# Moving one copy of weight sums to the row unit's loads, and one weight tile ahead of the last chunk's sums, in a decoder layer kernel

## Chip, cores and metric

The kernel runs on one core of one Trainium2 chip. The metric is the device time of one execution in microseconds (us). Engines are named as the profile names them: PE (matmul), DVE (VectorE), ACT (ScalarE), POOL (GpSimd), SP (SyncE, which here only issues DMAs).

## What is computed

A decoder layer on x of shape (1, 256, 1024) in float32. Two parallel head groups, a pooled mixer and a causal attention, share an input projection; then comes a cross-attention into 256 memory tokens; then a SwiGLU feed-forward with 2816 hidden columns. Each is followed by a layer norm. The change lies in the feed-forward:

```python
def swiglu(h, w_gate, w_up, w_down):
    return (jax.nn.silu(h @ w_gate) * (h @ w_up)) @ w_down

h = layer_norm(DEEPNORM_ALPHA * h + swiglu(h, w_gate[l], w_up[l], w_down[l]),
               ln3_g[l], ln3_b[l])
```

## The kernel before

**Two parts of every weight.** Float32 products are made from reduced-precision operands. Each weight tile w is split into a high part, `wNh`, an ACT cast of the raw tile `wNr` (L160), and a low part, `wNl`, a DVE subtraction raw minus high (L176). PE then does three products per pair: high by high, high by low, low by high (`three`, L484 to L486; for gate and up L499 and L505). So every weight tile passes SP (load), ACT (cast), DVE (subtract) and PE, in that order. The class `Stream` numbers the tiles 0 to 150 in the order of their use. A raw tile has one of 7 buffers, and SP loads the next tile as soon as DVE has subtracted the tile that held the buffer; split tiles have 10 slots at this stage. `ws.more()` casts and splits one tile ahead of its use, if a slot is free; while `ws.held` is true, nothing is split ahead on its own. `ws.before(n, load)` hangs another load in front of tile n's load on SP's queue.

**Saved products.** Several weight matrices are multiplied by a scheme with seven products of quarters instead of eight (names y, z, w and o are a tile's place in it). The scheme needs sums of weight quarters. DMAs make them in DRAM: `begin_sums(i)` (L435) copies a third of two quarters of down's weights, 1.5 MB, from the input to `sum_z`, and `begin_second(i)` (L440) copies 0.75 MB to `sum_w`, both on SP's queue. Then POOL issues two accumulating DMAs (`add_to`, L447): `add_first(i)` adds other quarters to `sum_z`, and `add_second(i)`, once the first has landed, adds `sum_z` to `sum_w`. `add_first(1)` is issued behind tile 97's cast, `add_first(2)` behind tile 112's cast (`behind`, L428, a small POOL addition that reads the tile). The copies' places are set by one table:

```python
for i, (at, then) in enumerate(((c_gu[1][0], c_gu[1][2]), (c_gs[0]["o"], c_gs[0]["w"]), (c_gu[9][2], c_gu[9][3]))):
    ws.before(at, lambda i=i: begin_sums(i))
    ws.before(then, lambda i=i: begin_second(i))
```

**The feed-forward's order.** Gate and up are done in 11 chunks of 256 columns. Chunks 1 to 4 and 7 to 10 have four tiles each and 64 matmuls (`proj_both`); chunk 10 has tiles 111 to 114, chunk 9 tiles 107 to 110. Chunks 5 and 6 are one "row unit" (`Rows.products`) in four groups with tiles 85 to 98; its third group has tiles 92 (y), 93 (o), 94 (w) and 95 (z), its fourth 96 to 98. After a chunk's matmuls, `Gated.add` takes its four results from PSUM: an ACT copy (L1349) and a DVE addition (L1350) each, called the chunk's sums here. While the next chunk's matmuls run, `multiply` (ACT silu L1354, DVE product L1355) and `split` (three DVE additions L734 to L736, an ACT cast L1368, a DVE subtraction L1375) make the chunk's input for down. Down's weights are tiles 115 to 150. Its first products, of tiles 115 and 116, use PSUM banks that chunk 9 has left; the products of tile 117 need banks that chunk 10's sums set free.

Every engine takes its instructions in the order of the program.

Of the kernel before, what the change touches and what calls it, by code (L numbers as in the profile page):

```python
# [24 lines left out]
NFC = DFF // CW  # L25
# [18 lines left out]
ROWS = (5, 6)  # L44
# [178 lines left out]
def decoder_layer(  # L223
# [78 lines left out]
    c_gu, c_gs = {}, [{} for _ in range(KD // 2)]  # L302
# [122 lines left out]
    def behind(number):  # L425

        hi = r32(ws.tiles[number][0][:, 0, 0:1])
        nc.gpsimd.tensor_add(token, hi, hi)  # L428
# [3 lines left out]
    def begin_sums(i):  # L432
        sums_begun.add(i)
        js = slice(i * THIRD, (i + 1) * THIRD)
        nc.sync.dma_start(sum_z[:, :, js], w_sum[:, 1:3, js])  # L435

    def begin_second(i):
        sums_begun.add(~i)
        js = slice(i * THIRD, (i + 1) * THIRD)
        nc.sync.dma_start(sum_w[:, js], w_sum[:, 1, js])  # L440

    for i, (at, then) in enumerate(((c_gu[1][0], c_gu[1][2]), (c_gs[0]["o"], c_gs[0]["w"]), (c_gu[9][2], c_gu[9][3]))):
        ws.before(at, lambda i=i: begin_sums(i))
        ws.before(then, lambda i=i: begin_second(i))

# [3 lines left out]
    def add_first(i):  # L449
        assert i in sums_begun  # L450
        js = slice(i * THIRD, (i + 1) * THIRD)
        add_to(sum_z[:, :, js], w_sum[:, 2:4, js])

    def add_second(i):
        assert ~i in sums_begun
        js = slice(i * THIRD, (i + 1) * THIRD)
        add_to(sum_w[:, js], sum_z[:, 1, js])
# [33 lines left out]
    def proj_both(pss, numbers, yT, group=KD):  # L491

        for k0 in range(0, KD, group):
            for k in range(k0, k0 + group):
                hi, _ = ws.get(numbers, k)
                for b, ps in enumerate(pss):
                    nc.tensor.matmul(ps, hi[:, b * P:(b + 1) * P], yT.both(k), start=k == 0, stop=False,  # L499
                                     skip_group_check=True)  # L500
                yield
            for k in range(k0, k0 + group):
                _, lo = ws.parts_of(numbers, k)
                for b, ps in enumerate(pss):
                    nc.tensor.matmul(ps[:, S:], lo[:, b * P:(b + 1) * P], yT.pair(k)[0], start=False,  # L505
                                     stop=k == KD - 1, skip_group_check=True)
                ws.done(numbers, k)
                if ws.pace == 1:
                    ws.next()
                yield  # L510
# [31 lines left out]
    def run(gen, n=None):  # L542

        while n is None or n > 0:
            if next(gen, gen) is gen:
                return False
            n = None if n is None else n - 1
        return True
# [778 lines left out]
    def gated_t():  # L1327
        pt = bank("pgt").rearrange("p (f t) -> p f t", f=2)
        for t in range(T):
            for f in range(2):  # L1330
                nc.tensor.transpose(pt[:, f, t * P:(t + 1) * P], sg0[:, t, f * P:(f + 1) * P], ident)
        gated_parts(0)
        split(gT[0][0], gT[0][1], pt.rearrange("p f (t s) -> p (f t) s", t=T))
# [179 lines left out]
    for c in range(1, NFC):  # L1513
        if c == ROWS[0]:
            run(more_forms)
            rows = Rows()
            ws.lazy = c_gu[ROWS[-1] + 1][2:]
            gu = rows.products()
            run(gu, 3)
            left.multiply()  # L1520
            run(gu, 5)
            ws.apart = True
            run(gu, 1)
            left.split()
            run(gu, 7)
            ws.held = True
            run(gu)
            behind(c_gs[3]["w"])
            add_first(1)
            add_second(1)  # L1530
            left = rows
        if c in ROWS:
            continue
        pss = [(accbank if c % 2 else bank)("pg") for _ in range(4)]
        if c == 3:
            ws.ahead += 1
            ws.widen("spare", sp)
            add_second(0)
        if c == 10:
            behind(c_gu[10][1])  # L1540
            add_first(2)
            add_second(2)
        ws.held = ws.held or c in (ROWS[0] - 1, NFC - 1)
        gu = proj_both(pss, c_gu[c], h2T, KD if c == 1 else 4)
        run(gu, 2)
        if left:
            left.multiply()
        if left and left is rows:
            ws.prepare(c_gu[c][-1] + 1)
        run(gu, 2)  # L1550
        if left and left is rows:
            run(gu, 3)
            left.transposed()
            left.split()
            ws.held = False
        elif left:
            left.split((more_forms, 4 - c) if c in (2, 3) else None)
            if c == 2:
                run(more_forms, 2)
            if c == ROWS[-1] + 2:  # L1560
                run(later)
        else:
            run(gu, 4)
            gated_t()
        if c >= 2:
            run(gu, 7 if c < ROWS[0] else 4 if c == ROWS[-1] + 1 else 0)
            if c < ROWS[0] - 1:
                run(more_forms, 1)
            if c == ROWS[0] - 1:
                ws.more()  # L1570
            ws.held = True
        run(gu)
        left = Gated(c, pss)
        left.add()
        ws.held = False
# [174 lines left out]
```

## Time and profile before

| | us |
|---|---|
| median of 3 runs (378.67, 379.5, 378.67) | 378.67 |
| the profiled execution's own time | 379.65 |
| its span in the profile | 377.9 |
| PE busy / DVE busy / ACT busy / POOL busy | 364.5 / 341.9 / 231.3 / 37.3 |

The profile is of one execution. Its times are from the start of the span; a row of a timeline has start, duration, engine, line, operation and tile, with the engine's idle time before it in brackets, and the engine that ended that. "DMA to landing" is the time from an issue to its completion. A matmul row is longer than the pitch between matmuls, since they are pipelined; the pitch is read from the starts. "q1" is the queue of the DMAs that SP issues, "q0" that of POOL's accumulating ones; both run on the core's 16 DMA engines.

### The profile page before, as it was taken

How to read it: one execution, taken by the hardware profiler on the slowest of the kernel's cores; microseconds unless marked ns; L12 is line 12 of the kernel's file. 1: busy time of each engine (PE TensorE's matmuls, PEld its weight loads, DVE VectorE, ACT ScalarE, POOL GpSimd, SP SyncE). 2: the span in 40 equal slices, each digit the busy share in tenths (PEclk: the TensorE clock that was granted, in tenths of full speed). 3: DMA queues.
4: the chain of work that ended last, by engine and by line, in shares of the span. 5: the costliest groups of instructions: out<-in, count | busy, mean ns of one | idle time of the engine just before them, and what ended most of it. 6: DMA issues, size and time to landing. Idle time of an engine off the chain costs nothing.

```text
span 377.9 us, 5500 instructions
## 1 busy us (share of the span) xinstructions
PE 364.5 (96%) x1941; PEld 309.2 (82%) x1941; DVE 341.9 (90%) x523; ACT 231.3 (61%) x356; POOL 37.3 (10%) x43
## 2 busy tenths in 40 slices
PE   8999999999999999999999999999999998899991
PEld 7887878888888899988888888888988875688880
DVE  5878998999999899899869999999977998999995
ACT  5767768658272865774467675775646475777611
POOL 0000145700130001001100000020000100000002
PEclk9999999999999999999999999999999999899997
DMA  7999999769869999999999996389999998899402
GB/s 267 414 409 357 236 366 289 273 234 294 342 117 257 377 361 340 245 363 343 264 248 333 375 316 209 114 280 230 370 327 378 211 325 290 274 367 301 180 0 112
DMA packets 33755, 107.58 MB, mean 285 GB/s; under 512 B 3264, under 2 KB 4544, under 8 KB 32320
## 3 DMA queue, kind: packets, MB, share of 16 engines
q1 hardware_dynamic: 31056, 93.41, 68.2%
q0 software_dynamic: 2240, 13.37, 18.3%
q10 hardware_dynamic: 432, 0.46, 0.3%
q8 instruction: 15, 0.25, 0.3%
q14 instruction: 12, 0.10, 0.1%
HBM read 106.18 MB, written 27.79 MB: 355 GB/s over the span
## 4 chain that ended last, share of the span: by engine, by line
PE 70%; DVE 16%; DMA 6%; issue 3%; ACT 3%; SPq 0%; DVEq 0%; ACTq 0%
PE pg L499 8%; PE pg L505 4%; PE pxq L499 4%; PE pxk L499 4%; PE pqk L618 4%; DMA w110r<-in_w_gu 3%; PE m L485 3%; PE m L486 3%; PE m L484 3%; PE x L484 2%; PE x L486 2%; PE x L485 2%; PE pxk L505 2%; PE pxq L505 2%; PE pu L499 2%
## 5 line engine op out<-in xcount | busy, mean ns | idle before, releaser
L1368 ACT CAST g<-sq 128x1024 fp32r<-128x1024 f32 x7 | 7.4, 1052 | 14.6 <-DVE sq L736 14.6
L923 POOL TENSOR_TENSOR rs<-mv,mhalf 128x1 f32<-128x1 f32 x6 | 3.8, 640 | 101.5 <-DVE mv L921 101.5
L683 ACT ACTIVATE pr<-pr,mx 128x128 f32<-128x128 f32 (+1 forms) x16 | 7.1, 445 | 7.7 <-DVE mx L714 7.7
L1375 DVE TENSOR_TENSOR g<-sq,g 128x1024 fp32r<-128x1024 f32 x7 | 8.6, 1224 | 1.1 <-ACT g L1368 1.1
L1354 ACT ACTIVATE sq<-sq 128x512 f32<-128x512 f32 x8 | 5.1, 640 | 5.4 <-DVE sq L1350 5.4
L912 DVE BATCH_NORM_STATS2 st<-r 128x6 f32<-128x512 f32 (+1 forms) x12 | 8.1, 671 | 0.4
L577 ACT ACTIVATE h2f<-tp,turned 128x128 f32<-128x128 f32 x8 | 3.0, 456 | 7.0 <-PE tp L574 7.0
L928 DVE SCALAR_TENSOR_TENSOR r<-r,mv,gb 128x512 f32<-128x512 f32 (+2 forms) x10 | 6.9, 726 | 0.1
L428 POOL TENSOR_TENSOR token<-w97h 128x1 f32<-128x1 f32 x1 | 1.0, 963 | 60.6 <-ACT w97h L160 60.6
L1349 ACT COPY sq<-pg 128x256 f32<-128x256 f32 x16 | 5.1, 371 | 2.6 <-DVE g L1375 1.3
L1350 DVE TENSOR_TENSOR sq<-pg,sq 128x256 f32<-128x256 f32 x16 | 6.0, 417 | 0.7 <-ACT sq L1349 0.7
L1029 DVE TENSOR_TENSOR r<-r,u 128x512 f32<-128x512 f32 x6 | 6.0, 1009 | 0.1
L826 ACT CAST xkTh<-pxk 128x256 fp32r<-128x256 f32 x8 | 2.6, 377 | 5.6 <-PE pxk L505 5.6
L1350 DVE TENSOR_TENSOR sg<-pg,sg 128x256 f32<-128x256 f32 x16 | 6.0, 414 | 0.0
L939 ACT ACTIVATE h<-r,rs 128x512 f32<-128x512 f32 x2 | 1.3, 716 | 7.3 <-DVE r L928 7.3
L1355 DVE TENSOR_TENSOR sq<-sq,sg 128x512 f32<-128x512 f32 x8 | 5.5, 687 | 0.3
L683 ACT ACTIVATE xpr<-xs,mx 128x256 f32<-128x256 f32 x6 | 2.8, 470 | 4.8 <-DVE mx L694 4.8
L783 POOL TENSOR_TENSOR win<-upad 128x542 f32<-128x542 f32 x2 | 4.0, 1994 | 16.3 <-DVE upad L816 16.3
L447 POOL DMA_DIRECT2D sum_w<-sum_z x3 | 2.6, 853 | 28.8 <-DMA sum_z<-in_w_sum 28.8
L1349 ACT COPY sg<-pg 128x256 f32<-128x256 f32 x16 | 5.3, 392 | 0.0
L1034 DVE TENSOR_TENSOR r<-m,r 128x512 f32<-128x512 f32 (+1 forms) x8 | 5.2, 649 | 0.1
L1113 PE MATMUL xs<-xkTh,xq 128*128 128x256 f32 x24 | 4.8, 282 | 0.0
(1375 smaller groups left out, 1395.2 us busy)
## 6 DMA issues: line engine op xcount, KB each, us to landing
sum_z<-in_w_sum SPq DMA_DIRECT2D x3, 1536.0 KB, 14.6
sum_z<-in_w_sum POOLq DMA_DIRECT2D x3, 1536.0 KB, 15.2
sum_w<-in_w_sum SPq DMA_DIRECT2D x3, 768.0 KB, 14.8
sum_w<-sum_z POOLq DMA_DIRECT2D x3, 768.0 KB, 9.8
gs_z<-in_w_gs SPq DMA_DIRECT2D x1, 2048.0 KB, 9.8
gs_z<-in_w_gs POOLq DMA_DIRECT2D x1, 2048.0 KB, 17.8
wr<-in_w_qkv SPq DMA_DIRECT2D x5, 256.0 KB, 5.6
mr<-in_mem_t SPq DMA_DIRECT2D x1, 1024.0 KB, 11.3
```

The costliest lines, as they stand in the source:

```text
L484: nc.tensor.matmul(ps, wa, ya, start=start, stop=False, skip_group_check=part)
L485: nc.tensor.matmul(ps, wa, yb, start=False, stop=False, skip_group_check=part)
L486: nc.tensor.matmul(ps, wb, ya, start=False, stop=stop, skip_group_check=part)
L499: nc.tensor.matmul(ps, hi[:, b * P:(b + 1) * P], yT.both(k), start=k == 0, stop=False, skip_group_check=True)
L505: nc.tensor.matmul(ps[:, S:], lo[:, b * P:(b + 1) * P], yT.pair(k)[0], start=False, stop=k == KD - 1, skip_group_check=True)
L618: nc.tensor.matmul(qk[i], part(i)[0], xT.both(k), start=first, stop=False, skip_group_check=True)
L683: nc.scalar.activation(dst[:, j, :], src[:, j, :], AF.Exp, bias=mx[:, j:j + 1], scale=sign, accum_out=sm[:, j:j + 1])
L912: nc.vector.bn_stats(self.st[:, self.n, :], self.r[:, c0:c1] if src is None else src)
L1349: nc.scalar.copy(y[:, f, :], ps[:, S:])
L1350: nc.vector.tensor_add(y[:, f, :], ps[:, :S], y[:, f, :])
L1368: nc.scalar.copy(hi[:, :n], q[:, :n])
L1375: nc.vector.tensor_sub(lo[:, :n], q[:, :n], r32(hi[:, :n]))
```

## The change

Two edits. The third pair of copies (i = 2) hangs no longer in front of tiles 109 and 110 (chunk 9), but in front of tiles 94 and 95 (the row unit's third group). And in chunk 10, `ws.more()` is called ahead of the point where the stream is held, as it was in chunk 4 only; it casts and splits tile 118.

```diff
-    for i, (at, then) in enumerate(((c_gu[1][0], c_gu[1][2]), (c_gs[0]["o"], c_gs[0]["w"]), (c_gu[9][2], c_gu[9][3]))):
+    for i, (at, then) in enumerate(((c_gu[1][0], c_gu[1][2]), (c_gs[0]["o"], c_gs[0]["w"]), (c_gs[2]["w"], c_gs[2]["z"]))):
         ws.before(at, lambda i=i: begin_sums(i))
         ws.before(then, lambda i=i: begin_second(i))
...
-            if c == ROWS[0] - 1:
+            if c in (ROWS[0] - 1, NFC - 1):
                 ws.more()
             ws.held = True
```

On SP's queue, at the row unit's third group, stands now (w92r to w96r are raw tiles, `in_w_gs`, `gs_w` and `gs_z` the row unit's weights and their sums in DRAM):

```order
 L108 DMA w92r<-in_w_gs 128x2x512
 L108 DMA w93r<-in_w_gs 128x1024
+L435 DMA sum_z<-in_w_sum 256x1x1536
 L105 DMA w94r<-gs_w 128x512
+L440 DMA sum_w<-in_w_sum 128x1536
 L108 DMA w95r<-gs_z 128x2x512
 L108 DMA w96r<-in_w_gs 128x2x512
```

The two copies come ahead of tiles 94 and 95; the tiles' own order is as it was.

On the same queue at chunk 9 (`in_w_gu` are gate's and up's weights) stands:

```order
 L108 DMA w107r<-in_w_gu 128x1024
 L108 DMA w108r<-in_w_gu 128x1024
-L435 DMA sum_z<-in_w_sum 256x1x1536
 L108 DMA w109r<-in_w_gu 128x1024
-L440 DMA sum_w<-in_w_sum 128x1536
 L108 DMA w110r<-in_w_gu 128x1024
 L108 DMA w111r<-in_w_gu 128x1024
```

Tiles 109 and 110 follow tile 108 with nothing between.

On DVE at the end of chunk 10 (`go` is chunk 9's input for down, `sq` and `sg` on `pg` are chunk 10's sums) stands:

```order
 L176 TENSOR_TENSOR w117l<-w117r,w117h 128x1024
 L1375 TENSOR_TENSOR go<-sq,go 128x512
-L1350 TENSOR_TENSOR sq<-pg,sq 128x256 x2
-L1350 TENSOR_TENSOR sg<-pg,sg 128x256 x2
 L176 TENSOR_TENSOR w118l<-w118r,w118h 128x1024
+L1350 TENSOR_TENSOR sq<-pg,sq 128x256 x2
+L1350 TENSOR_TENSOR sg<-pg,sg 128x256 x2
 L165 TENSOR_TENSOR w120r<-w119r,w120r 128x512
 L176 TENSOR_TENSOR w119l<-w119r,w119h 128x1024
 L176 TENSOR_TENSOR w120l<-w120r,w120h 128x1024
-L1355 TENSOR_TENSOR sq<-sq,sg 128x512
 L176 TENSOR_TENSOR w121l<-w121r,w121h 128x1024
```

Tile 118's subtraction passes the four sums; behind it the stream stays one tile further ahead, so that chunk 10's product L1355 follows tile 121 and its additions L734 to L736 follow tile 123. ACT's casts move in the same way. The instructions are the same in number on every engine.

## The prediction

> **What bounds the kernel now.** I read the page first, then busy time by stretch, the chain of waits, and the timelines of DVE, PE and SP around the change.
>
> ```profile
> span 377.9 us, 5500 instructions
> ```
>
> Busy time by stretch (stretch; sum of PE, PE's weight loads, DVE, ACT, POOL with counts; granted clock; share of the 16 DMA engines; GB/s):
>
> ```profile
> 228.00:250.00 22.00, 22.00 (x121) 19.15 (x120) 21.23 (x31) 15.12 (x22) 0.00 (x0) 1.00 0.55 170
> 280.00:290.00 10.00, 10.00 (x60) 8.92 (x60) 4.96 (x8) 3.79 (x4) 0.00 (x0) 1.00 1.02 397
> 310.00:320.00 10.00, 9.13 (x36) 6.27 (x36) 8.82 (x14) 5.82 (x8) 0.00 (x0) 1.00 0.92 266
> 320.00:326.00 6.00, 3.68 (x9) 2.69 (x10) 6.00 (x7) 3.88 (x5) 0.00 (x0) 0.73 0.73 250
> 326.00:358.00 32.00, 32.00 (x141) 26.27 (x140) 30.92 (x30) 23.51 (x25) 0.00 (x0) 1.00 0.86 299
> ```
>
> Four things are to be seen. The DMA engines are full in 280 to 290, in chunk 9, and little over half used in 228 to 250, around the row unit's start. In 280 to 290 DVE works only 4.96 of 10 us, while PE does not feel it yet. PE pays later: in 310 to 326 it starts 45 matmuls in 16 us, where at the pace of 326 to 358 (141 in 32 us, 0.227 us each) 45 take 10.2 us. So 5.8 us of PE is lost there, partly as waits, partly as a clock of 0.73. And in 326 to 358 DVE is busy 30.92 of 32 us: it has no spare time in which to catch up.
>
> The chain of waits, asked for 264 to 324, has the load of tile 110 as its longest piece, with its cast behind it; asked for the whole span, it goes on with tile 150's subtraction and DVE's work of the last norm to the end (start, duration, what):
>
> ```profile
> 273.35 12.67 DMA w110r<-in_w_gu
> 286.04 1.06 ACT w110h L160
> ```
>
> ```profile
> 357.15 1.22 DVE w150l L176
> 358.37 0.60 DVE r L1008
> ...
> 372.52 0.75 DVE r L933
> ```
>
> DVE's timeline shows what the late tiles hold up:
>
> ```profile
> 284.02 1.23 DVE L176 TENSOR_TENSOR w109l<-w109r,w109h 128x1024 fp32r<-128x1024 f32 x1 [3.10 <-ACT w109h L160]
> 287.12 1.23 DVE L176 TENSOR_TENSOR w110l<-w110r,w110h 128x1024 fp32r<-128x1024 f32 x1 [1.87 <-ACT w110h L160]
> 309.36 0.75 DVE L1350 TENSOR_TENSOR sq<-pg,sq 128x256 f32<-128x256 f32 x2
> 310.69 1.21 DVE L176 TENSOR_TENSOR w118l<-w118r,w118h 128x1024 fp32r<-128x1024 f32 x1
> 311.82 0.68 DVE L165 TENSOR_TENSOR w120r<-w119r,w120r 128x512 f32<-128x512 f32 x1
> ```
>
> Tiles 109 and 110 land late, behind the third pair of copies on the same queue, and DVE idles 3.10 + 1.87 = 4.97 us. From there on DVE is behind PE and is the path: it reaches chunk 10's sums at 309.36, and from 311.82 on it runs almost without a gap, and at the end its work of the norm follows on tile 150's.
>
> **The copies leave chunk 9.** Landing times of the copies (first two lines: the second pair, with only loads beside it; next two: the third pair), of tile 108, and the slowest load in the whole trace; then each queue's bytes in MB and share in 274 to 280, when POOL's accumulate is on the engines too:
>
> ```profile
> sum_z<-in_w_sum SPq DMA_DIRECT2D x1, 1536.0 KB, 9.4
> sum_w<-in_w_sum SPq DMA_DIRECT2D x1, 768.0 KB, 11.3
> ...
> sum_z<-in_w_sum SPq DMA_DIRECT2D x1, 1536.0 KB, 14.6
> ...
> sum_w<-in_w_sum SPq DMA_DIRECT2D x1, 768.0 KB, 16.5
> ...
> w108r<-in_w_gu SPq DMA_DIRECT2D x1, 512.0 KB, 7.3
> ...
> w73r<-in_w_gu SPq DMA_DIRECT2D x1, 512.0 KB, 21.4
> ```
>
> ```profile
> q0 software_dynamic: 139, 0.78, 63.3%
> q1 hardware_dynamic: 198, 0.94, 40.1%
> ```
>
> ```profile
> 266.59 0.33 SPq L108 DMA_DIRECT2D w108r<-in_w_gu  x1
> ```
>
> Tile 108 lands at 266.59 + 7.3 = 273.9. Without copies, tiles 109 and 110 (0.52 MB each) come next. The loads' queue moved 0.94 MB in 274 to 280, so both are down at about 280.5. DVE wants 109 at 284.02 - 3.10 = 280.9 and 110 one subtraction later, each with a cast of 1.06 us before it. So little or nothing of the 4.97 us is left, and I take nothing; 1 us of it could stay at no cost, as comes next.
>
> **What is late next: PE.** PE runs dense through chunk 10, and its end does not move. PE's and DVE's rows of chunk 4 show how long after the start of the last eight matmuls a chunk's sums can begin; then the last eight of chunk 10:
>
> ```profile
> 240.87 1.12 PE L505 MATMUL pg<-h2T,w84l 128*128 128x256 f32 x8
> ...
> 305.34 1.12 PE L505 MATMUL pg<-h2T,w114l 128*128 128x256 f32 x8
> ```
>
> ```profile
> 242.07 0.76 DVE L1350 TENSOR_TENSOR sq<-pg,sq 128x256 f32<-128x256 f32 x2 [0.18 <-ACT sq L1349]
> 242.75 0.75 DVE L1350 TENSOR_TENSOR sg<-pg,sg 128x256 f32<-128x256 f32 x2
> ```
>
> That is 242.07 - 240.87 = 1.20 us, so chunk 10's sums begin no sooner than 305.34 + 1.20 = 306.54. DVE would be there at 309.36 - 4.97 = 304.39, and would wait 2.15 us.
>
> **Tile 118 ahead of the sums** fills 1.13 us of that wait (310.69 to 311.82): DVE arrives at 305.52, 1.02 us early. This is the slack that a rest of the old stall could use up. ACT's cast of 118 passes the sums likewise, in time in which ACT, too, waits for PE. If the old stall stayed whole, the same subtraction would only put the sums 1.13 us later and cover nothing, at no change in DVE's total.
>
> **The sum.** In chunk 4 the four additions end at 242.75 + 0.75 = 243.50, 1.43 us after their start. So chunk 10's end at 306.54 + 1.43 = 307.97, and the addition for tile 120, which begins at 311.82 now, begins there: 3.85 us earlier. Behind it stand the same instructions (L1355 and L734 to L736 in other places among them), with PE ahead of DVE's needs and every load issued when DVE frees a buffer; I carry the 3.85 us to tile 150 and, since the chain there is DVE's, through the last norm. PE could give 5.8 us, so DVE sets the gain. The profiled execution's own time is 379.65, its span 377.9: 1.75 us lie around the span and stay. 379.65 - 3.85 = 375.8. The profiled execution is 0.98 us above the median of the runs; from the median, 378.67 - 3.85 = 374.8.
>
> **The copies come to the row unit.** SP issues `sum_z` behind tile 93 and `sum_w` behind tile 94; DVE and ACT want tiles 94 and 95 here:
>
> ```profile
> 227.99 0.33 SPq L108 DMA_DIRECT2D w93r<-in_w_gs  x1
> ...
> 233.59 0.52 SPq L108 DMA_DIRECT2D w95r<-gs_z  x1
> ```
>
> ```profile
> 246.12 0.69 DVE L165 TENSOR_TENSOR w94r<-w92r,w94r 128x512 f32<-128x512 f32 x1
> 249.60 1.22 DVE L176 TENSOR_TENSOR w95l<-w95r,w95h 128x1024 fp32r<-128x1024 f32 x1
> 255.72 1.22 DVE L176 TENSOR_TENSOR w98l<-w98r,w98h 128x1024 fp32r<-128x1024 f32 x1
> ```
>
> ```profile
> 257.72 0.39 PE L485 MATMUL g<-w98l,extra 128*128 128x512 f32 x1
> ```
>
> The copies start at about 228.4 and, just ahead of tile 95, at 232.9. By the landings 9.4 to 14.6 and 11.3 to 16.5 they are down at 237.8 to 243.0 and 244.2 to 249.4, and the tile behind each 1.3 us later (0.52 MB at 397 GB/s): 94 at 239.1 to 244.3, before 246.12; 95 at 245.5 to 250.7, needed by 249.60 less a cast, 248.54. I take the lower ends, since the share of the DMA engines here is 0.55, with loads alone as beside the second pair; cost nothing. At the upper end DVE is 2.2 us late, PE has 257.72 - 255.72 - 1.22 = 0.78 us of slack at tile 98, and 1.4 us of the gain goes. The two issues delay SP by under a microsecond; behind them tiles 94 and 95 wait for buffers anyway. That cover gone, they would cost that once. On POOL nothing changes place; its third accumulate still waits for tile 112's cast, long after the copies.
>
> **Rivals.** *Part of it only*, 376.2: either the upper end just worked out (3.85 - 1.4 = 2.45), or PE becomes the bound. PE still waits for DVE, 5.8 - 3.85 = 1.95 us in all. In 310 to 326 it idled 0.87 + 2.32 = 3.2 us in several pieces, and the clock in 320 to 326 was 0.73, a loss of 6 x 0.27 = 1.6 us; one such dip fits into 1.95, two cost 1.25, a gain of 2.6. [...]
>
> *Nothing*, 377.9: the sums' last accumulate now starves tile 117. POOL issues it behind tile 112's cast, so about 5 us sooner:
>
> ```profile
> 293.20 1.05 POOL L447 DMA_DIRECT2D sum_z<-in_w_sum  x1 [0.15 <-issue]
> 304.78 0.86 POOL L447 DMA_DIRECT2D sum_w<-sum_z  x1 [10.54 <-DMA sum_z<-in_w_sum]
> ```
>
> ```profile
> 300.71 0.68 DVE L165 TENSOR_TENSOR w117r<-w115r,w117r 128x512 f32<-128x512 f32 x1
> ```
>
> ```profile
> q0 software_dynamic: 193, 1.19, 96.3%
> q1 hardware_dynamic: 45, 0.09, 4.6%
> ```
>
> The accumulate takes 11.6 us, and in 296 to 302 the loads got 4.6% beside it (0.09 MB). Now 288.2 to 299.8. DVE wants tile 117 at 300.71 - 4.97 = 295.7. Held to 299.8, less the slack of 1.0, it costs 3.05 us: gain 0.8. Against it: 117's load is issued behind tile 110's subtraction, ahead of tile 112's cast, now as before, and the row of 300.71 has no wait. [...] Beside it stands that the change doesn't do what it says: the accumulate alone holds tiles 109 and 110 as long as before, which its 0.94 MB contradicts; 378.7.
>
> *Slower*, 380.5: the row unit starves. If tile 95 takes as long as the slowest load, 21.4 us, from its issue at 233.6, it lands at 255.0, and its subtraction starts at 256.05, 6.45 us late. Less 0.78, PE loses 5.67 us at tile 98, chunk 10 ends that much later, and 5.67 - 3.85 = 1.8 us are lost. It counts as slower from a delay of 0.78 + 3.85 + 1.1 = 5.75 us. Against it stands the share of 0.55.
>
> **Chances.** Forecast 0.74, part 0.10, nothing 0.11 (of which starved 0.07), slower 0.05. A measurement tells about 0.3% (1.1 us) from no change: faster 0.84, same 0.11, slower 0.05. The range runs from 373.7 (all 4.97 us) to 376.6 (part, plus half the runs' spread of 0.83); it holds forecast and part, 0.84.
>
> **What would show it.** Right: DVE without a wait over 1 us at tiles 109 and 110; a wait of about 1 us in front of chunk 10's sums, which begin near 306.5; tile 120's addition near 308.0; tile 150's subtraction near 353.3; PE dense to 306. Wrong: an idle PE in 241 to 261, a DVE wait at 117, sums begun after 307.5, or PE's clock low in more than one dip.

## The result, and the profile after

The changed kernel takes 374.0 us in the median (373.91 to 375.24), against 378.67: a ratio of 0.9879, 95% interval [0.9854, 0.9903]. That is 4.67 us less, where 3.85 were forecast.

The page of after, and its busy time by stretch (columns as before):

```profile
span 372.3 us, 5497 instructions
```

```profile
228.00:250.00 22.00, 22.00 (x121) 19.15 (x120) 21.30 (x30) 15.12 (x22) 0.00 (x0) 1.00 0.85 286
280.00:290.00 10.00, 10.00 (x61) 8.90 (x60) 9.86 (x17) 6.00 (x10) 1.51 (x2) 1.00 0.86 277
310.00:320.00 10.00, 9.05 (x40) 7.07 (x39) 8.81 (x11) 5.99 (x7) 0.00 (x0) 1.00 0.90 290
320.00:326.00 6.00, 6.00 (x27) 4.74 (x26) 5.97 (x8) 3.89 (x4) 0.00 (x0) 1.00 0.92 324
```

The DMA engines' share has gone from 0.55 to 0.85 in 228 to 250, and from 1.02 to 0.86 in 280 to 290; PE is full in both. DVE works 9.86 of 10 us in 280 to 290 in place of 4.96. In 310 to 326 PE starts 67 matmuls, not 45, at full clock.

DVE's timeline of after, at the places named in the prediction:

```profile
278.22 1.22 DVE L176 TENSOR_TENSOR w108l<-w108r,w108h 128x1024 fp32r<-128x1024 f32 x1
...
279.96 1.22 DVE L176 TENSOR_TENSOR w109l<-w109r,w109h 128x1024 fp32r<-128x1024 f32 x1
281.09 1.22 DVE L176 TENSOR_TENSOR w110l<-w110r,w110h 128x1024 fp32r<-128x1024 f32 x1
...
305.63 0.76 DVE L1350 TENSOR_TENSOR sq<-pg,sq 128x256 f32<-128x256 f32 x2 [1.07 <-ACT sq L1349]
...
306.97 0.68 DVE L165 TENSOR_TENSOR w120r<-w119r,w120r 128x512 f32<-128x512 f32 x1
...
351.92 1.23 DVE L176 TENSOR_TENSOR w150l<-w150r,w150h 128x1024 fp32r<-128x1024 f32 x1
```

The waits at tiles 109 and 110 are gone; a wait of 1.07 us stands in front of chunk 10's sums. To set this against before, one row of before is needed, tile 108's, ahead of all that the change touches on DVE there:

```profile
279.10 1.22 DVE L176 TENSOR_TENSOR w108l<-w108r,w108h 128x1024 fp32r<-128x1024 f32 x1
```

At tile 108 this execution is already 0.88 us ahead. It is so from long before the change's first instruction, and other executions stand elsewhere (0.28 to 1.07 us ahead in the traces below whose tile 108 nothing holds up), so it is scatter. I therefore compare distances that start at tile 108. From there to tile 120's addition it is 311.82 - 279.10 = 32.72 us before and 306.97 - 278.22 = 28.75 after: 3.97 us less. To tile 150 it is 357.15 - 279.10 = 78.05 before and 351.92 - 278.22 = 73.70 after: 4.35 less.

The copies and tile 95 in the row unit: landing times, then tile 95 on SP and on DVE.

```profile
sum_z<-in_w_sum SPq DMA_DIRECT2D x1, 1536.0 KB, 9.3
sum_w<-in_w_sum SPq DMA_DIRECT2D x1, 768.0 KB, 9.4
w95r<-gs_z SPq DMA_DIRECT2D x1, 512.0 KB, 10.0
```

```profile
232.69 0.56 SPq L108 DMA_DIRECT2D w95r<-gs_z  x1
```

```profile
248.70 1.22 DVE L176 TENSOR_TENSOR w95l<-w95r,w95h 128x1024 fp32r<-128x1024 f32 x1
```

Tile 95 lands at 232.69 + 10.0 = 242.7 and its cast of 1.06 us is wanted at 247.6: 4.9 us to spare. Its subtraction stands 0.90 us ahead of before's, as tile 108's does. The row unit pays nothing.

### The profile page after: what moved, and what is told of

Its sections match the earlier page's. It is cut to its first block, busy times and chain, and to the rows that moved or that the text cites. A ratio compares the mean times of both kernels' runs of the same rounds, so it can differ in the third digit from the quotient of the medians.

```text
span 372.3 us, 5497 instructions
## 1 busy us (share of the span) xinstructions
PE 362.4 (97%) x1941; PEld 308.1 (83%) x1941; DVE 341.5 (92%) x523; ACT 230.8 (62%) x356; POOL 37.4 (10%) x43
## 4 chain that ended last, share of the span: by engine, by line
PE 85%; DVE 6%; DMA 3%; issue 2%; ACT 2%; POOL 1%; POOLq 0%; ACTq 0%; DVEq 0%
PE pg L499 16%; PE pg L505 8%; PE pxq L499 4%; PE pxk L499 4%; PE pqk L618 4%; PE m L485 3%; PE m L486 3%; PE m L484 3%; PE x L484 2%; PE x L485 2%; PE x L486 2%; PE pxk L505 2%; PE pxq L505 2%; PE pu L499 2%; PE xv L484 2%; PE pqk L621 2%
## 5 line engine op out<-in xcount | busy, mean ns | idle before, releaser
L1375 DVE TENSOR_TENSOR g<-sq,g 128x1024 fp32r<-128x1024 f32 x7 | 8.6, 1223 | 1.1 <-ACT g L1368 1.1
L428 POOL TENSOR_TENSOR token<-w97h 128x1 f32<-128x1 f32 x1 | 1.0, 968 | 61.5 <-ACT w97h L160 61.5
L1355 DVE TENSOR_TENSOR sq<-sq,sg 128x512 f32<-128x512 f32 x8 | 5.5, 687 | 0.3
```

The source lines that it names most:

```text
L1375: nc.vector.tensor_sub(lo[:, :n], q[:, :n], r32(hi[:, :n]))
```

## The experiments

For each kernel, the time and its ratio to before on the same chip, and from its trace DVE's distance from tile 108 to tile 150, worked out as above (before 78.05). Four chips were used, and before takes 378.8 to 379.3 us on them, so times of kernels that ran on different chips compare to about 0.5 us.

| kernel | us | ratio, interval | 108 to 150 |
|---|---|---|---|
| before, again | 378.92 | 0.9991 [0.9973, 1.0009] | 77.60 |
| tile 118 ahead alone | 377.22 | 0.996 [0.9945, 0.9976] | 76.95 |
| copies alone | 376.69 | 0.9942 [0.9928, 0.9955] | 76.35 |
| copies alone, norm's load later | 375.72 | 0.9899 [0.988, 0.9917] | 75.85 |
| copies alone, tile ahead behind the sums | 375.71 | 0.9898 [0.988, 0.9916] | 74.94 |
| changed, again | 374.3 | 0.988 [0.9865, 0.9895] | 73.43 |
| changed, one copy more | 374.06 | 0.9854 [0.9827, 0.9882] | 73.55 |
| changed, accumulate earlier | 373.79 | 0.9848 [0.9828, 0.9868] | 73.38 |
| two tiles ahead | 373.02 | 0.9845 [0.9831, 0.9859] | 72.49 |
| three tiles ahead | 373.03 | 0.9838 [0.9812, 0.9865] | 72.54 |
| copies at chunk 8 | 378.78 | 0.9996 [0.9978, 1.0015] | |
| changed, three copies more | 384.26 | 1.0122 [1.0087, 1.0158] | |

The last two are late at tile 108 already, so the distance doesn't hold their loss.

**The copies alone.** Against the changed kernel:

```diff
-            if c in (ROWS[0] - 1, NFC - 1):
+            if c == ROWS[0] - 1:
```

> Only the copies move, tile 118 stays behind chunk 10's sums. My theory: the copies leaving chunk 9 free the sums, PE's end of chunk 10 then sets their start (305.6 in the changed kernel's trace), and tile 118's subtraction of 1.13 us, now behind the sums, is paid in full. DVE waits 1.07 + 1.13 = 2.2 us in front of the sums, which begin at the same place, and the time is 374.0 + 1.1 = 375.1 us. First rival, tile 118's place gives nothing (DVE has time to spare behind the sums): 374.0. Second rival, the two edits need each other and the copies alone give little: above 377.

376.69: the copies give 2.1 of the 4.5 us, and what tile 118 adds is 2.4 us, twice my 1.1. DVE's rows of this kernel:

```profile
306.24 0.76 DVE L1350 TENSOR_TENSOR sq<-pg,sq 128x256 f32<-128x256 f32 x2 [2.22 <-ACT sq L1349]
...
308.01 1.23 DVE L176 TENSOR_TENSOR w118l<-w118r,w118h 128x1024 fp32r<-128x1024 f32 x1 [0.35 <-ACT w118h L160]
...
328.67 0.69 DVE L165 TENSOR_TENSOR w131r<-w129r,w131r 128x512 f32<-128x512 f32 x1 [0.96 <-DMA w131r<-sum_w]
...
340.44 1.23 DVE L176 TENSOR_TENSOR w138l<-w138r,w138h 128x1024 fp32r<-128x1024 f32 x1 [0.39 <-ACT w138h L160]
```

The sums stand where PE puts them, with the 2.22 us wait forecast. But three more waits show: 0.35 for tile 118's cast, which ACT now makes behind its copies of the sums, 0.96 for tile 131's load, some 20 us later, and 0.39 at tile 138. The longer wait at the sums (2.22 in place of 1.07) and these three make 2.85 us; the traces' distances differ by 2.92 from the changed kernel's second trace (76.35 - 73.43), the medians by 2.4. SP's queue shows the wait at tile 131. First this kernel, then the changed one, then tile 131's landing time in each:

```profile
319.05 0.38 SPq L108 DMA_DIRECT2D w129r<-in_w_sum  x1
...
320.53 0.42 SPq L386 DMA_DIRECT2D gb<-in_ln_b  x1
321.35 0.33 SPq L105 DMA_DIRECT2D w131r<-sum_w  x1
```

```profile
313.53 0.38 SPq L108 DMA_DIRECT2D w129r<-in_w_sum  x1
...
319.10 0.33 SPq L105 DMA_DIRECT2D w131r<-sum_w  x1
```

```profile
w131r<-sum_w SPq DMA_DIRECT2D x1, 256.0 KB, 7.3
```

```profile
w131r<-sum_w SPq DMA_DIRECT2D x1, 256.0 KB, 3.9
```

Tile 129 takes the buffer of tile 122, which is free once tile 124's addition (L165, `w124r<-w122r,w124r`) has read it. DVE's rows of that addition and of L1375, the last step of chunk 10's input for down, again in this kernel and then in the changed one:

```profile
317.16 1.23 DVE L1375 TENSOR_TENSOR g<-sq,g 128x1024 fp32r<-128x1024 f32 x1 [1.12 <-ACT g L1368]
318.30 0.68 DVE L165 TENSOR_TENSOR w124r<-w122r,w124r 128x512 f32<-128x512 f32 x1
```

```profile
312.79 0.69 DVE L165 TENSOR_TENSOR w124r<-w122r,w124r 128x512 f32<-128x512 f32 x1
...
316.71 1.23 DVE L1375 TENSOR_TENSOR g<-sq,g 128x1024 fp32r<-128x1024 f32 x1 [1.12 <-ACT g L1368]
```

In before's order the addition stands behind L1375 and its wait of 1.1 us for ACT; with the stream a tile further ahead it stands in front of both. So tiles 129 and 130 and the norm's load leave SP some 5 us earlier, and tile 131 is issued 319.10 - 315.02 = 4.08 us behind the norm's load in place of 0.82: it lands at 319.10 + 3.9 = 323.0 in place of 321.35 + 7.3 = 328.7.

**Tile 118 alone.** Against the changed kernel:

```diff
-    ..., (c_gs[2]["w"], c_gs[2]["z"]))):
+    ..., (c_gu[9][2], c_gu[9][3]))):
```

> Only tile 118 moves ahead of chunk 10's sums, the copies stay in chunk 9. My theory: DVE is late at the sums here, so the tile covers no wait; it makes the sums begin 1.13 us later (309.36 + 1.13 = 310.5 by the trace of before) and what stands behind them is where it was: 378.7 us, within 1.1 of it. DVE's waits at tiles 109 and 110 stay at about 5 us together. Rival, the tile alone carries part of the gain: 377.5 or less. Other rival, later sums hold PE's first products of down: 379.8 or more.

377.22: faster by 0.9 to 2.1 us (the interval), where I expected none. The sums are not what gained, as DVE's rows show:

```profile
307.78 1.22 DVE L176 TENSOR_TENSOR w118l<-w118r,w118h 128x1024 fp32r<-128x1024 f32 x1
308.92 0.75 DVE L1350 TENSOR_TENSOR sq<-pg,sq 128x256 f32<-128x256 f32 x2
...
328.64 0.68 DVE L165 TENSOR_TENSOR w131r<-w129r,w131r 128x512 f32<-128x512 f32 x1
```

The sums follow tile 118 without a wait, so it fills nothing there; tile 131 has none either.

**Before, again**, unedited, for a second trace.

> The kernel before the change once more, for a second trace of it: 378.8 us, within 0.8. The tile alone gained 1.6 us where I expected none. In its trace the addition for tile 131 and the subtraction of tile 138 don't wait, where the first trace of before shows 0.20 and 0.39 us; with the copies alone tile 131 waits 0.96. Theory: the tile ahead brings the loads of tiles 129 to 131 forward, and before's wait at tile 131 is often longer than its first trace shows: here 0.5 to 1.2 us. Rival, before's waits behind chunk 10 are again about 0.6 us together, and most of the 1.6 us lies elsewhere.

```profile
329.22 0.69 DVE L165 TENSOR_TENSOR w131r<-w129r,w131r 128x512 f32<-128x512 f32 x1 [0.73 <-DMA w131r<-sum_w]
```

The wait at tile 131 is 0.73 us here (0.20 in the first trace), as the theory wants; tile 138 waits 0.4 in both, and not with the tile ahead. That is 0.6 to 1.1 us of the tile's own gain; the interval of 0.9 to 2.1 reaches into that, and what may lie above it is not settled. This trace also has shorter waits at tiles 109 and 110, 2.36 and 1.73, in all 4.09 in place of 4.97; with the tile alone they are 4.46. Without these waits the distance from tile 108 to tile 150 is 73.08 and 73.51 in before's two traces and 72.49 with the tile: by the traces, too, the tile alone gains 0.6 to 1.0 us.

**The tile ahead, but behind the sums.** Against the copies alone:

```diff
         ws.held = False
-    ws.next()
+    ws.more(2)
```

> As the copies alone, but the stream is put one tile further ahead right behind chunk 10's sums in place of ahead of them: tile 118 passes nothing, while from tile 121 on the order is that of the changed kernel. It splits what the tile ahead is worth beside the moved copies (2.4 us: 374.3 against 376.7). Theory: DVE still waits 2.2 us in front of the sums and 0.35 for tile 118's cast (1.1 to 1.5 us lost against the changed kernel), the wait at tile 131 (0.96) is gone: 375.6, within 0.4. Rival, all lies in the fill ahead of the sums: 376.7. Other rival, all lies in the order behind: 374.3.

375.71, as expected. Its rows:

```profile
307.93 1.23 DVE L176 TENSOR_TENSOR w118l<-w118r,w118h 128x1024 fp32r<-128x1024 f32 x1 [0.35 <-ACT w118h L160]
```

The wait at the cast stays, those at tiles 131 and 138 are gone. So the tile's gain splits into the fill ahead of the sums and the order behind them. By the traces' distances the fill is worth 74.94 - 73.43 = 1.5 us and the order 76.35 - 74.94 = 1.4. By the medians it is 1.4 and 1.0, but this kernel ran on another chip than the other two; by each kernel's gain over before on its own chip it is 1.0 and 1.4. Both parts are there, at 1.0 to 1.5 us each; which is larger is not settled.

**The norm's load one place later.** Against the copies alone:

```diff
-    ws.before(c_dn[5]["w"], load_norm("b", 3, ln3_b))
+    ws.before(c_dn[5]["z"], load_norm("b", 3, ln3_b))
```

> As the copies alone, with the norm's second load of 0.52 MB one place later on the queue, behind tile 131's load in place of ahead of it. Nothing else moves. Theory: tile 131's wait of 0.96 us is that load, standing in front of it, and its loss goes to the end: 376.7 - 1.0 = 375.7. Rival, DVE has time to spare behind tile 131, or the next tile's load is late in its place: 376.7.

```profile
330.57 1.23 DVE L176 TENSOR_TENSOR w132l<-w132r,w132h 128x1024 fp32r<-128x1024 f32 x1 [0.47 <-ACT w132h L160]
```

The norm's load was in tile 131's way: without it there, tile 131 doesn't wait. But the next tile, now behind that load, waits 0.47 us for its cast. The median is the expected one, but on another chip than the copies alone; by the traces only 76.35 - 75.85 = 0.5 us is won.

**The changed kernel, again**, unedited.

> The changed kernel once more, beside the others on the same chip: 374.0 us, within 0.4. If the 0.8 us by which it beat the forecast of 3.85 is only scatter, its gain here is nearer to 3.85 than to 4.67.

The gain is 4.5 us, by the interval 4.0 to 5.1: more than the forecast 3.85, so the surplus is not all scatter.

**Two tiles ahead, and three.** Against the changed kernel:

```diff
-                ws.more()
+                ws.more(2 if c == NFC - 1 else 1)
```

and with 3 in place of 2.

> As the changed kernel, with tile 119 (and tile 120's addition ahead of it, 0.60 + 1.13 us on DVE) also ahead of chunk 10's sums. My theory: DVE still waits 1.07 us in front of the sums; this work of 1.73 us fills the wait and makes the sums 0.66 us later. DVE's chain behind it gains 1.07, unless PE sets it from there, which it nearly does (326 to 353: PE busy 26.23 of 27 us, DVE 26.28): 373.0 to 374.0. Rival, the later sums and with them the later end of the gate's product hold PE: 374.7 or more.

> As the kernel with two tiles ahead of chunk 10's sums, with a third one, tile 120 (1.13 us on DVE), ahead of them too. With two ahead DVE no longer waits in front of the sums (they began at 306.61, right behind tile 119) and PE waits for nothing between 300 and 345. Theory: a tile ahead pays only as long as there is a wait for it to fill; here there is none, so the sums begin 1.13 us later and the time stays at 373.0, within 0.5. Rival, each tile ahead gains about 1 us, as the first two did: 372.0. Other rival, the late sums hold PE: 373.9 or more.

DVE's rows with two ahead:

```profile
305.48 1.22 DVE L176 TENSOR_TENSOR w119l<-w119r,w119h 128x1024 fp32r<-128x1024 f32 x1
306.61 0.75 DVE L1350 TENSOR_TENSOR sq<-pg,sq 128x256 f32<-128x256 f32 x2
```

The rest of the wait is filled and the time falls by another 1.3 us, to 373.02; its interval [0.9831, 0.9859] lies below the changed kernel's [0.9865, 0.9895] on the same chip. The third tile changes nothing (373.03): no wait in front of the sums is left for it to fill. In both kernels DVE waits 0.39 us at tile 138 again, so the order that two or three tiles ahead make is not free of that wait.

**The copies at chunk 8.** Against the changed kernel:

```diff
-    ..., (c_gs[2]["w"], c_gs[2]["z"]))):
+    ..., (c_gu[8][2], c_gu[8][3]))):
```

> As the changed kernel, but the third copies stand ahead of tiles 105 and 106 (chunk 8), where the second accumulate fills the DMA engines and loads land 12.1 to 12.8 us after their issue in the changed kernel's trace. My theory: a place is free only where the engines have room; here 2.36 MB at the 321 GB/s of 260 to 270 make the tiles behind them 7.3 us later, against slacks of 3.6 to 4.8 us at tiles 105 to 107. DVE waits 3 to 5 us in all at tiles 105 to 110, less the 1.07 in front of the sums: 376 to 378 us. Rival, anywhere ahead of chunk 9 is as good: 374.0.

```profile
274.64 1.23 DVE L176 TENSOR_TENSOR w105l<-w105r,w105h 128x1024 fp32r<-128x1024 f32 x1 [0.82 <-ACT w105h L160]
281.37 1.22 DVE L176 TENSOR_TENSOR w106l<-w106r,w106h 128x1024 fp32r<-128x1024 f32 x1 [5.51 <-ACT w106h L160]
```

378.78: the whole gain is lost. The mechanism is the one I named, a stall of 0.82 + 5.51 = 6.3 us, larger than my 3 to 5. What the change does well is the place, not that the copies leave chunk 9.

**More copies in the row unit**, one and three. Against the changed kernel:

```diff
+    spares = [dram.tile([P, 2, THIRD, 512], F32, name=f"spare{n}") for n in range(1)]
...
-        nc.sync.dma_start(sum_z[:, :, js], w_sum[:, 1:3, js])
+        for to in [sum_z[:, :, js]] + spares * (i == 2): nc.sync.dma_start(to, w_sum[:, 1:3, js])
```

and with `range(3)`.

> As the changed kernel, with the third copy of 1.57 MB made once more beside it in the row unit, into a buffer that nothing reads. My theory: tile 95 landed at 242.7 in the changed kernel and its cast is wanted at 247.6, so the row unit has 4.9 us of room; 1.57 MB at 397 GB/s take 4.0 us, tile 95 lands near 246.7, DVE waits nowhere over 1 us there: 374.0 us, within 1.1. Rival, the row unit was full with the one pair (share of the DMA engines 0.85 in 228 to 250): 376 or more.

With one more, tile 95's landing time:

```profile
w95r<-gs_z SPq DMA_DIRECT2D x1, 512.0 KB, 14.0
```

4.0 us later, as worked out, and the time stays at 374.06. The row unit had room for two thirds more bytes than the pair's 2.36 MB.

> As the changed kernel, with the third copy of 1.57 MB made three times more, 4.72 MB, into buffers that nothing reads. This is the slower case of the prediction, made on purpose. My theory: 11.9 us more of transfers, so tile 95 lands near 254.6 in place of 242.7 and DVE waits 7.0 us for its cast; PE has 0.78 us of slack at tile 98 and loses about 6.2 us: 380.2 us, slower than before the change. Rival, the loss is hidden because DVE catches up ahead of chunk 9: 376 or less.

```profile
254.36 0.69 DVE L165 TENSOR_TENSOR w94r<-w92r,w94r 128x512 f32<-128x512 f32 x1 [8.27 <-DMA w94r<-gs_w]
...
258.94 1.23 DVE L176 TENSOR_TENSOR w95l<-w95r,w95h 128x1024 fp32r<-128x1024 f32 x1 [1.02 <-ACT w95h L160]
```

384.26, slower than before and 4 us more than I said. I had priced tile 95 alone, but the extra copies stand ahead of tile 94 too, and DVE stops at its addition first, for 8.27 + 1.02 = 9.3 us in all. What reaches the end is PE's loss, as PE's waits in the row unit and DVE's row at chunk 10's sums show:

```profile
256.24 0.79 PE L485 MATMUL g<-w93l,h2T 128*128 128x512 f32 x1 [3.23 <-DVE w93l L176]
...
264.08 0.50 PE L485 MATMUL g<-w97l,extra 128*128 128x512 f32 x1 [1.63 <-DVE w97l L176]
...
266.35 0.79 PE L485 MATMUL g<-w98l,extra 128*128 128x512 f32 x1 [1.31 <-DVE w98l L176]
```

```profile
316.89 0.76 DVE L1350 TENSOR_TENSOR sq<-pg,sq 128x256 f32<-128x256 f32 x2 [1.45 <-ACT sq L1349]
```

At the sums DVE waits for PE by 1.45 us, more than in the changed kernel, so PE is what is late there. It idles 3.23 + 1.63 + 1.31 = 6.2 us, as much as I said. But its clock also falls, to a mean of 0.57 in 256 to 260 and again in 266 to 270, and each time eight matmuls take 3.5 us from first start to the next behind them, in place of 1.8. PE's time from the row unit's first matmul to chunk 7's first grows from 19.1 us (240.93 to 260.00 in the changed kernel) to 29.6 (241.71 to 271.27): 10.5 us, near the 10.3 of the medians (384.26 - 374.0). The waits at tile 94 and the clock are what I left out.

**The accumulate earlier.** Against the changed kernel:

```diff
-            behind(c_gu[10][1])
+            behind(c_gu[9][2])
```

> As the changed kernel, but POOL issues the third accumulate behind tile 109's cast in place of tile 112's, about 7.5 us earlier (near 279.7), on top of the loads of tiles 113 to 118. This sharpens the prediction's case in which the accumulate starves tile 117. My theory: loads beside an accumulate land in 12 to 13 us, as tiles 104 to 107 did beside the second one; tile 117, issued at 282.34, lands near 295 and DVE wants it at 294.7, so DVE waits under 1 us and that is covered by the 1.07 in front of the sums: 374.0 us, within 1.1. Rival, the loads get next to nothing beside it (4.6% of the engines' time, as in 296 to 302 of before): tile 117 lands after 292, with tiles 114 to 116 ahead of it late as well, DVE waits 4 us or more: 376.5 or more.

POOL's row of the accumulate, and SP's of the two loads:

```profile
282.73 1.03 POOL L447 DMA_DIRECT2D sum_z<-in_w_sum  x1
```

```profile
282.42 0.33 SPq L105 DMA_DIRECT2D w117r<-sum_w  x1
284.54 0.53 SPq L108 DMA_DIRECT2D w118r<-sum_z  x1
```

The accumulate was issued 4.4 us earlier than in the changed kernel (287.17), not 7.5, since POOL's small addition L428 ahead of it took 4.43 us (0.46 in the changed kernel). So it stands just behind tile 117's load, which lands after 6.3 us, in time; tile 118's, behind it, takes 12.5 us, to 297.0, with its cast wanted at 302. 373.79: no DVE wait comes of it. The load behind the accumulate was slow, as feared: 12.5 us, against 6.3 for tile 117's, ahead of it. What it would cost with the accumulate ahead of tile 117's load wasn't tried.

## Why the prediction was right, point by point

- *The stall at 109 and 110 goes*: right. Both come without a wait on DVE. Its size, 4.97 us, was that of one execution, 0.98 us above the median; another had 4.09.
- *PE's end of chunk 10 is next, at 306.54*: right. The sums begin at 305.63 in an execution that is 0.88 ahead: 306.51.
- *Tile 118 fills 1.13 us and leaves 1.02*: 1.07 was left. Without it the loss is 1.5 by the rows (2.22 - 1.07 + 0.35), not 1.13, since its cast, too, then waits behind ACT's copies of the sums.
- *Tile 120's addition 3.85 us earlier*: 3.97.
- *The copies cost nothing in the row unit*: right, with 4.9 us to spare; one more copy beside them was free. The landings that the range was built on were those of the second and third pair; the first pair, beside an accumulate, had taken 19.3 and 14.8 us in before, which the working left out. With 9.3 and 9.4 measured it did no harm.
- *Carried to the end unchanged, L1355 and L734 to L736 "in other places among them"*: this is the step that was mis-sized. The new order behind the sums is worth something of its own, since additions that free buffers now stand ahead of a product that waits for ACT. It removes before's waits at tiles 131 and 138, 0.6 us in one trace of before and 1.1 in the other; beside the moved copies it is worth 1.0 to 1.4. I had costed it at nothing, having seen that the instructions were the same in number, and not asked who waits for the buffers that they free. With it the first trace gives 3.85 + 0.6 = 4.4 us.
- *How near the number came* is in part luck. The same working on before's second trace, with its shorter stall, gives only 3.0 us: the last eight matmuls of chunk 10 start at 304.31, tile 120's addition would begin at 304.31 + 1.20 + 1.43 = 306.94, and it began at 309.94. With that trace's 1.1 it comes to 4.1. The 4.67 and 4.5 measured lie a little above both sums; that rest is within the intervals and not explained.
- *Rivals.* Part of it only: the changed kernel shows no dip of PE's clock in 310 to 326, and with the norm's load later, where DVE was the path, a dip cost nothing that shows (below). Starved: the load behind the accumulate was slow in the run above (12.5 us), but tile 117's stands ahead of it, as the prediction argued, and DVE had no wait for it. The 4.6% is not the share of loads that wait all the time: in before tile 118 landed at 290.49 + 5.2 = 295.7 and the next load was issued at 296.81, so part of 296 to 302 had no load to move; in 302 to 303, with loads waiting, their queue had 31 of 62 packets and 19.0%. Slower: it exists with three times the bytes, it enters at tile 94, and PE's clock adds to it (its threshold of 5.75 adds up to 5.73).

## What to carry to other kernels

A copy that can be made at any time belongs where the loads behind it have room; count that room in us from a tile's landing to its first use, for every tile behind the copy (4.9 us at tile 95 here), and test it with one more copy. Work pulled ahead of a wait paid up to that wait and no further (the second tile 1.3 us, the third nothing), so fill it and stop there. And when an edit shifts an in-order stream by one place, go through what each shifted instruction frees: a load that left some 5 us earlier took away a wait of 0.96 us here, some 20 us behind the edit.

## What the runs showed of the hardware

PE's clock dipped after idle pieces that were each short, 1.56 and 0.95 us. With tile 118 alone, PE's last waits ahead of the dip, and the clock of the stretch, 0.72:

```profile
320.94 0.51 PE L484 MATMUL m<-w124h,g 128*128 128x512 f32 x1 [1.56 <-ACT w124h L160]
...
322.39 0.79 PE L485 MATMUL m<-w124l,g 128*128 128x512 f32 x1 [0.95 <-DVE w124l L176]
```

```profile
320.00:326.00 6.00, 4.11 (x10) 3.08 (x11) 5.98 (x6) 4.63 (x5) 0.00 (x0) 0.72 0.89 313
```

With the tile ahead behind the sums, the same two waits are 1.43 and 0.95 us, and with the copies at chunk 8 they are 1.57 and 0.94; in both the clock stays at 1.00 in 320 to 326 (over the whole span its mean is 0.992 in both, and 0.988 with the tile alone). So the lengths of the two pieces alone do not decide; what does is not shown. Where DVE was the path, a dip cost nothing that shows: with the norm's load later, PE had a clock of 0.53 in the same stretch, and DVE was busy 5.98 of its 6 us. Where PE was the path it cost: 1.7 us for each of the two dips with three more copies.

In two stretches beside an accumulate, with loads outstanding on their queue, the two queues moved as many packets, 80 and 84 each, but not as many bytes. Packets, MB and share of each queue in 261 to 264 of the changed kernel, and then in 291 to 294 of the kernel with the accumulate earlier:

```profile
q0 software_dynamic: 80, 0.49, 79.7%
q1 hardware_dynamic: 80, 0.27, 24.5%
```

```profile
q0 software_dynamic: 84, 0.52, 83.9%
q1 hardware_dynamic: 84, 0.17, 17.2%
```

A packet of the accumulate carries 6.1 and 6.2 KB here and one of the loads 3.4 and 2.0; the loads got 24.5% and 17.2% of the engines' time. The counts are not equal throughout: in 288 to 291 of the second kernel, with tile 118's load outstanding, they are 89 and 65.
